# Block sums of the last feed-forward product and the last additions of the second norm: VectorE or GpSimd

## The chip, the cores and the metric

The kernel runs on one core of a Trainium2 chip. The metric is the device time of one execution in microseconds (us). Lower is better. Before the change, three executions took 989.52, 991.27 and 992.14 us; their median is 991.27 us.

## The reference, cut to what matters

One post-norm decoder layer over 1024 tokens of 1024 channels in float32. The pooling and attention mixers come first; what the change touches comes after them:

```python
h = layer_norm(DEEPNORM_ALPHA * h + mix, ln1_g[i], ln1_b[i])

ff = jnp.square(jax.nn.relu(h @ w_ff1[i])) @ w_ff2[i]          # (1024,1024)@(1024,4096)@(4096,1024)
h = layer_norm(DEEPNORM_ALPHA * h + ff, ln2_g[i], ln2_b[i])     # the second norm: (x-mean)*rstd*g + b

gate = jax.nn.sigmoid(h @ w_ple_gate[i] + b_ple_gate[i])
h = h + gate * (p[i] @ w_ple[i])
```

## The kernel before, in words

**Products in three parts.** Each float32 operand is split into a high part (a cast to `fp32r` on ScalarE, `high`, L98) and a low part (the operand minus its high part, `low`, L103, on VectorE nearly everywhere). `mm3` (L112 to L115) multiplies high by high, high by low and low by high into one PSUM bank, so each 128x512 block product is three matmuls: L113, L114, L115.

**The feed-forward's second product** is done by a Strassen-like scheme of seven products (`SEQUENCE` = 1, 5, 4, 3, 7, 6, 2). Each product runs over eight groups of hidden channels (`QORDER`), which gives 56 units, numbered 0 to 55 here. A unit is 24 matmuls of 512 columns. For unit u, `prepare(u)` makes both operands: the activation operand is a sum or a difference of two hidden blocks for the products whose first entry in `PRODUCTS` has two parts (a tile `st`, 128x1024 floats, two buffers), then split into a tile `w` (two buffers). The weight operand is read into a tile `ws`, and split into one half of a tile `x_703` (two halves in turn). `multiply(u)` then runs the 24 matmuls. The last product, number 2, is units 48 to 55, and each of its units has such a sum.

In the rows below the sums and splits of the late units are: unit 46 `st_6503`, `w_6505`; 47 `st_6536`, `w_6538`; 48 `st_6584`, `w_6586`, weights `ws_6501`; 49 `st_6617`, `w_6619`, `ws_6534`; 50 `st_6654`, `w_6656`; 51 `st_6702`; 52 `st_6750`; 53 `st_6792`; 54 `st_6855`; 55 `st_6897`.

**The second norm** (`norm2`, `layer_norm`) works on a block of 128 tokens. Statistics on VectorE (L403, L405), reciprocal root (L409 and L410 for blocks 0 to 3, GpSimd's `pow` at L412 for blocks 4 to 7), the mean taken off on ScalarE (L418), the scaling by gain on VectorE (L419), and last the addition of the bias `gb[1]` (tile `ws_6344`). Blocks 0 to 3 lie in the tile `pre_5033`, and their norms run while products 6 and 2 are multiplied; blocks 4 to 7 (`n_5251`, `n_5253`, `n_6733`, `n_6735`) follow product 2. After a block's norm, `flip` transposes it: a 32x32 transpose on VectorE (L424), a write to DRAM (L425, SP's queue) and four reads back (L427, SP's queue). The result is split and multiplied with the gate weights.

**What sets the order.** Each engine runs its instructions in the order that the scheduler of the framework gave them when the program was built; an instruction that waits holds up all behind it on its engine. GpSimd's queue also issues the transfers of L740, which add one weight block onto another.

Of the kernel before, what the change touches and what calls it, by code (L numbers as in the profile page):

```python
# [10 lines left out]
ALU = mybir.AluOpType  # L11
# [56 lines left out]
def layer(ctx, tc, xT, x, pT, w_in, w_pool, pscale, sinks, w_out, ln1, w1, w2, ln2, w_ple, w_gate, bgate, bias, rcount, out):  # L68
    nc = tc.nc
# [13 lines left out]
    def wt(shape, dt=F32R):  # L83
        return sb.tile(shape, dt, tag="w", bufs=2, name=nm("w"))
# [4 lines left out]
    def stage(shape):  # L89
        return sb.tile(shape, F32, tag="st", bufs=2, name=nm("st"))  # L90

    def small(shape):
        return cp.tile(shape, F32, tag="sm", bufs=10, name=nm("sm"))
# [23 lines left out]
    def add(o, a, b, op=ALU.add):  # L117
        nc.vector.tensor_tensor(out=o, in0=a, in1=b, op=op)  # L118
# [278 lines left out]

    hn = [None] * NT

    def layer_norm(y, gb, root=False):  # L400
        st = small([P, 2, 6])
        for i in range(2):
            nc.vector.bn_stats(out=st[:, i, :], in_=y[:, i * HALF : (i + 1) * HALF])  # L403
        mv = small([P, 8])
        nc.vector.bn_aggr(out=mv[:, 0:2], in_=st.rearrange("p a b -> p (a b)"))  # L405
        v, r0, e, r, m = (mv[:, i : i + 1] for i in range(2, 7))
        nc.vector.tensor_scalar(out=v, in0=mv[:, 1:2], scalar1=LN_EPS, scalar2=None, op0=ALU.add)
        if root:
            nc.vector.reciprocal(out=r0, in_=v)  # L409
            nc.scalar.activation(out=r0, in_=r0, func=AF.Sqrt)  # L410
        else:
            nc.gpsimd.tensor_tensor(out=r0, in0=v, in1=mhalf, op=ALU.pow)  # L412

        nc.vector.scalar_tensor_tensor(out=e, in0=r0, scalar=v, in1=r0, op0=ALU.mult, op1=ALU.mult)
        nc.vector.tensor_scalar(out=e, in0=e, scalar1=-0.5, scalar2=1.5, op0=ALU.mult, op1=ALU.add)
        nc.vector.tensor_tensor(out=r, in0=r0, in1=e, op=ALU.mult)
        nc.vector.tensor_scalar(out=m, in0=mv[:, 0:1], scalar1=-1.0, scalar2=None, op0=ALU.mult)
        nc.scalar.activation(out=y, in_=y, func=AF.Identity, bias=m, scale=1.0)  # L418
        nc.vector.scalar_tensor_tensor(out=y, in0=y, scalar=r, in1=gb[0], op0=ALU.mult, op1=ALU.mult)  # L419
        add(y, y, gb[1])  # L420

    def flip(y, b, t, d):
        b4 = b.rearrange("p (q k c) -> p q k c", q=4, k=NK)
# [115 lines left out]
    def norm1(n):  # L539
        t, c = n // 4, n % 4  # L540
        layer_norm(hn[n], gb1)
        a = transposed(hn[n], 0, tr_ps())
        b = transposed(hn[n], 1, tr_av())
        nc.scalar.mul(out=hn[n], in_=hn[n], mul=ALPHA)
        nc.scalar.dma_start(out=h_dram[n], in_=hn[n])
        if t == 0:
            if c < 3:
                nc.scalar.copy(out=pre[:, 4 + c].rearrange("p (k t) -> p k t", k=4), in_=a)
            split_to("11", c, a, nc.vector)
            split_to("21", c, b, nc.vector)  # L550
        else:
            r12, t1, t2 = temp((P, 4, P)), temp((P, 4, P)), nat([P, 4, P])
            nc.scalar.copy(out=r12, in_=a)
            if c < 3:
                add(t1, a, pre[:, 4 + c].rearrange("p (k t) -> p k t", k=4), ALU.subtract)
            else:
                for i in range(2):
                    add(t1, t1 if i else a, block("11", i, c), ALU.subtract)
            add(t2, b, t1, ALU.subtract)
            split_to("22", c, b, nc.vector)  # L560
            add(r12, b, r12, ALU.subtract)
            split_to("T1", c, t1, nc.vector)
            split_to("T2", c, t2, nc.vector)
            diff[c] = t2, split_to("T3", c, r12, nc.vector)
# [159 lines left out]
    def incoming(shape=(P, 2, HALF)):  # L724
        return part(shape, F32)
# [44 lines left out]
    def hid(q, t, k):  # L770
        return hidden[q][:, k, t] if q in hidden else FF[q, k, t]

    SIGN = {1: ALU.add, -1: ALU.subtract}
    right = wide("x7", [P, 2, 2, 2, HALF], F32R)

    def split2(s, src):
        high(s[:, 0], src)
        lows.append(low(nc.vector, s[:, 1], src, s[:, 0]))
        return s

    def prepare(u):
        i, q = units[u]
        ta = PRODUCTS[i][0]
        a = hid(q, *ta[0][:2])
        if len(ta) == 2:
            sa = stage([P, 2, HALF])
            add(sa, a, hid(q, *ta[1][:2]), SIGN[ta[1][2]])
            a = sa
        b = blocks[u]
        if len(b) == 2:  # L790
            add(b[0], b[0], b[1], ALU.subtract)
        operands[u] = split2(wt([P, 2, 2, HALF]), a), split2(right[:, u % 2], b[0])
# [11 lines left out]
    acc = []  # L804
# [36 lines left out]
        return h2  # L841

    def norm2(n):
        layer_norm(acc[n], gb2, n < 4)

    def residual_back(count):
        for n in range(len(acc), len(acc) + count):
            acc.append(nat([P, D]))
            nc.sync.dma_start(out=acc[n], in_=h_dram[n])

    prepare(0)
    banks_of, pending = {}, []
    for u, (i, q) in enumerate(units):
# [13 lines left out]
        if u + 1 < len(units):  # L867
            prepare(u + 1)
# [13 lines left out]
        if i == 6:  # L882
            if k == 0:
                gb2 = [incoming((P, D)) for _ in range(2)]
                for j in range(2):
                    nc.sync.dma_start(out=gb2[j], in_=ln2[j].partition_broadcast(P))
            if k in (3, 6):
                norm2(k // 3 - 1)
        if i == 2:
            if k in (1, 4):  # L890
                norm2(2 + k // 3)
            if k == 2:
                residual_back(2)
            if k >= 2:
                gate_load(k - 2)
            if k == 4:
                gate_flip(0)
# [5 lines left out]
    for n in range(4, NT):  # L903
        norm2(n)
# [88 lines left out]
```

## Time and profile before

| | before |
|---|---|
| median of three executions | 991.27 us (989.52 to 992.14) |
| profiled execution, its own time | 990.92 us |
| its span, first to last instruction | 989.1 us |
| TensorE (PE) busy | 980.2 us, 99% |
| VectorE (DVE) busy | 718.7 us, 73% |
| ScalarE (ACT) busy | 457.6 us, 46% |
| GpSimd (POOL) busy | 106.7 us, 11% |
| TensorE clock granted | 1.0 throughout |

The time outside the span is 990.92 - 989.1 = 1.8 us. The shares are means over the span. PE counts as busy while matmuls follow each other in its pipeline, so its idle time is read from the starts of consecutive matmuls: 512 columns start every 0.23 us where nothing holds them.

### The profile page before, as it was taken

What the parts mean: (1) busy time and instruction counts of PE and PEld (TensorE: products, weight loads), DVE (VectorE), ACT (ScalarE), POOL (GpSimd) and SP (SyncE); (2) the same over time, 40 slices, a digit from 0 to 9 for tenths busy, and PEclk for the clock granted to TensorE, in tenths of its full rate; (3) what the DMA queues carried; (4) which work ended last, traced back from release to release, by engine and by line L of the source; (5) the groups of instructions that cost most, each with busy time, mean ns of one, the idle gap of its engine ahead of it and who ended that gap; (6) DMA issues with size and microseconds to landing.
All of it is one profiled execution on the core that took longest, in us unless ns stands there. A gap on an engine that the chain in (4) does not pass through costs nothing.

```text
span 989.1 us, 12163 instructions
## 1 busy us (share of the span) xinstructions
PE 980.2 (99%) x4498; PEld 814.0 (82%) x4498; DVE 718.7 (73%) x1137; ACT 457.6 (46%) x729; POOL 106.7 (11%) x142
## 2 busy tenths in 40 slices
PE   9999999999999999999999999999999999999998
PEld 7888887888888888888888888888888888778887
DVE  5798888895869777565446856887657699899533
ACT  5676666543576434444353433433434354553111
POOL 0013552020010000100000000100011110001000
PEclk9999999999999999999999999999999999999999
DMA  6512142622161543652363893675798776652411
GB/s 219 182 64 86 44 149 86 213 84 108 64 225 74 191 149 128 201 182 107 106 246 138 318 337 110 167 238 192 204 219 195 193 177 206 211 170 104 152 43 43
DMA packets 44763, 156.39 MB, mean 158 GB/s; under 512 B 5408, under 2 KB 10656, under 8 KB 41888
## 3 DMA queue, kind: packets, MB, share of 16 engines
q1 hardware_dynamic: 35280, 124.29, 36.6%
q0 software_dynamic: 7840, 26.74, 11.3%
q10 hardware_dynamic: 1584, 4.59, 1.2%
q8 instruction: 35, 0.57, 0.2%
q14 instruction: 24, 0.20, 0.1%
HBM read 128.86 MB, written 26.74 MB: 157 GB/s over the span
## 4 chain that ended last, share of the span: by engine, by line
PE 89%; DVE 5%; DMA 3%; issue 1%; ACT 1%; SPq 0%; DVEq 0%; ACTq 0%
PE f L114 20%; PE f L115 20%; PE f L113 20%; PE mm L113 8%; PE mm L115 8%; PE mm L114 8%; DMA ws<-in_w_gate 1%; DVE x L103 1%; PE pt L317 1%; DVE w L103 1%; PE s L294 1%; DMA ws<-in_w 1%; PE s L293 1%; DVE st L118 1%; PE av L323 1%
## 5 line engine op out<-in xcount | busy, mean ns | idle before, releaser
L114 PE MATMUL f<-x,w 128*128 128x512 f32 x448 | 174.8, 390 | 1.4 <-DVE x L103 1.2
L113 PE MATMUL f<-c,ws 128*128 128x512 f32 (+1 forms) x456 | 175.7, 385 | 0.0
L114 PE MATMUL f<-c,ws 128*128 128x512 f32 (+1 forms) x456 | 175.7, 385 | 0.0
L115 PE MATMUL f<-c,ws 128*128 128x512 f32 (+1 forms) x456 | 174.9, 386 | 0.0
L115 PE MATMUL f<-x,w 128*128 128x512 f32 x448 | 174.4, 389 | 0.0
L113 PE MATMUL f<-x,w 128*128 128x512 f32 x448 | 147.1, 389 | 0.0
L98 ACT CAST w<-st 128x1024 fp32r<-128x1024 f32 (+2 forms) x66 | 65.6, 998 | 104.0 <-issue 58.0
L103 DVE TENSOR_TENSOR w<-st,w 128x1024 fp32r<-128x1024 f32 (+2 forms) x66 | 77.4, 1176 | 44.6 <-ACT w L98 44.4
L114 PEld LDWEIGHTS f<-x,w 128*128 128x128 f32 x448 | 84.1, 188 | 20.7 <-DVE x L103 3.3
L115 PEld LDWEIGHTS f<-c,ws 128*128 128x128 f32 x456 | 85.7, 188 | 17.5 <-DVE ws L103 0.4
L114 PEld LDWEIGHTS f<-c,ws 128*128 128x128 f32 x456 | 85.7, 188 | 17.2
L113 PEld LDWEIGHTS f<-c,ws 128*128 128x128 f32 x456 | 85.7, 188 | 17.2
L113 PEld LDWEIGHTS f<-x,w 128*128 128x128 f32 x448 | 84.0, 188 | 17.6 <-ACT x L98 0.2
L115 PEld LDWEIGHTS f<-x,w 128*128 128x128 f32 x448 | 84.1, 188 | 17.3
L98 ACT CAST ws<-w 128x512 fp32r<-128x512 f32 x60 | 37.1, 622 | 57.8 <-PE f L115 42.4
L103 DVE TENSOR_TENSOR x<-ws,x 128x1024 fp32r<-128x1024 f32 x52 | 63.3, 1218 | 0.0
L118 DVE TENSOR_TENSOR n<-t,f 128x512 f32<-128x512 f32 x48 | 31.8, 684 | 39.3 <-PE f L115 39.2
L103 DVE TENSOR_TENSOR ws<-w,ws 128x512 fp32r<-128x512 f32 x60 | 41.1, 688 | 24.8 <-ACT ws L98 24.4
L98 ACT CAST ws<-st 128x512 fp32r<-128x512 f32 x48 | 29.8, 621 | 60.5 <-PE f L115 35.2
L113 PE MATMUL mm<-c,w 128*128 128x512 f32 x144 | 56.7, 399 | 0.2 <-ACT w L98 0.2
L115 PE MATMUL mm<-c,w 128*128 128x512 f32 x144 | 56.6, 394 | 0.0
L114 PE MATMUL mm<-c,w 128*128 128x512 f32 x144 | 56.5, 393 | 0.0
(210 smaller groups left out, 1811.9 us busy)
## 6 DMA issues: line engine op xcount, KB each, us to landing
ws<-in_w SPq DMA_DIRECT2D x70, 512.0 KB, 3.8
w<-in_w SPq DMA_DIRECT2D x16, 1024.0 KB, 5.0
c<-fd SPq DMA_DIRECT2D x6, 2048.0 KB, 8.6
fd<-n POOLq DMA_DIRECT2D x20, 512.0 KB, 3.5
ws<-in_w POOLq DMA_DIRECT2D x20, 512.0 KB, 7.9
st<-in_w_in SPq DMA_DIRECT2D x17, 512.0 KB, 3.3
w<-in_w SPq DMA_DIRECT2D x10, 512.0 KB, 4.1
n<-in_x SPq DMA_DIRECT2D x8, 512.0 KB, 5.7
```

The costliest lines, as they stand in the source:

```text
L98: nc.scalar.copy(out=dst, in_=src)
L103: return eng.tensor_tensor(out=dst, in0=src, in1=hi.bitcast(F32), op=ALU.subtract)
L113: nc.tensor.matmul(o, ah, bh, start=first, stop=False, skip_group_check=more)
L114: nc.tensor.matmul(o, ah, bl, start=False, stop=False, skip_group_check=more)
L115: nc.tensor.matmul(o, al, bh, start=False, stop=last, skip_group_check=more)
L118: nc.vector.tensor_tensor(out=o, in0=a, in1=b, op=op)
L293: nc.tensor.matmul(s[:, i, dst], ql, kt[:, 0, g, kk : kk + kn], start=True, stop=False)
L294: nc.tensor.matmul(s[:, i, dst], ql, kt[:, 1, g, kk : kk + kn], start=False, stop=True)
L317: nc.tensor.transpose(pt[:, i, :], e[:, i, kb * P : (kb + 1) * P], ident)
L323: nc.tensor.matmul(av, VV[0][:, blk, g], pp[:, 1], start=False, stop=(kb == 1))
```

## The change

Two kinds of 128x1024 additions are given to GpSimd: the sums of hidden blocks for product 2 (eight, L787), and the bias additions of the second norm (eight, L420). All others stay on VectorE; those of the first norm go through the same line of `layer_norm` with VectorE as the default.

```diff
-    def layer_norm(y, gb, root=False):
+    def layer_norm(y, gb, root=False, eng=None):
...
-        add(y, y, gb[1])
+        (eng or nc.vector).tensor_tensor(out=y, in0=y, in1=gb[1], op=ALU.add)
...
         if len(ta) == 2:
             sa = stage([P, 2, HALF])
-            add(sa, a, hid(q, *ta[1][:2]), SIGN[ta[1][2]])
+            (nc.gpsimd if i == 2 else nc.vector).tensor_tensor(out=sa, in0=a, in1=hid(q, *ta[1][:2]), op=SIGN[ta[1][2]])
             a = sa
...
     def norm2(n):
-        layer_norm(acc[n], gb2, n < 4)
+        layer_norm(acc[n], gb2, n < 4, nc.gpsimd)
```

GpSimd's queue, the difference, from its last L740 transfer on (`ws_6467`): the sums are `st_...`, the bias additions `pre_5033`.

```order
 L740 DMA ws_6467<-in_w 128x1024
+L420 TENSOR_TENSOR pre_5033<-pre_5033,ws_6344 128x1024
+L787 TENSOR_TENSOR st_6584<-n_4580,n_4561 128x1024
+L420 TENSOR_TENSOR pre_5033<-pre_5033,ws_6344 128x1024
+L787 TENSOR_TENSOR st_6617<-n_4830,n_4795 128x1024
+L420 TENSOR_TENSOR pre_5033<-pre_5033,ws_6344 128x1024 x2
+L787 TENSOR_TENSOR st_6654<-c_4886 128x1024
+L787 TENSOR_TENSOR st_6702<-c_4923 128x1024
+L787 TENSOR_TENSOR st_6750<-c_4959 128x1024
```

The queue was empty here up to the `pow` of block 4; now the sums of units 48 and 49 stand between bias additions, and those of units 50 on stand behind all four.

VectorE's queue before, from the scaling of block 2 (`sm_6688`) to the transpose of block 2 (`n_7052`):

```order
L419 SCALAR_TENSOR_TENSOR pre_5033<-pre_5033,sm_6688,ws_6343 128x1024
L103 TENSOR_TENSOR w_6586<-st_6584,w_6586 128x1024
L415 TENSOR_SCALAR sm_6826<-sm_6826 128x1
L103 TENSOR_TENSOR x_703_4878<-ws_6501,x_703_4878 128x1024
L424 STREAM_TRANSPOSE n_6943<-pre_5033 128x1024
L118 TENSOR_TENSOR pre_5033<-pre_5033,ws_6344 128x1024
L118 TENSOR_TENSOR st_6654<-c_4886 128x1024
L416 TENSOR_TENSOR sm_6826<-sm_6826 128x1
L103 TENSOR_TENSOR w_6619<-st_6617,w_6619 128x1024
L103 TENSOR_TENSOR x_703_4878<-ws_6534,x_703_4878 128x1024
L419 SCALAR_TENSOR_TENSOR pre_5033<-pre_5033,sm_6826,ws_6343 128x1024
L424 STREAM_TRANSPOSE n_7052<-pre_5033 128x1024
```

The same place with the change, from the split of unit 47 to that of unit 49:

```order
L103 TENSOR_TENSOR w_6538<-st_6536,w_6538 128x1024
L416 TENSOR_TENSOR sm_6688<-sm_6688 128x1
L416 TENSOR_TENSOR sm_6826<-sm_6826 128x1
L103 TENSOR_TENSOR x_703_4878<-ws_6467,x_703_4878 128x1024
L419 SCALAR_TENSOR_TENSOR pre_5033<-pre_5033,sm_6688,ws_6343 128x1024
L419 SCALAR_TENSOR_TENSOR pre_5033<-pre_5033,sm_6826,ws_6343 128x1024
L424 STREAM_TRANSPOSE n_6943<-pre_5033 128x1024
L103 TENSOR_TENSOR w_6586<-st_6584,w_6586 128x1024
L103 TENSOR_TENSOR x_703_4878<-ws_6501,x_703_4878 128x1024
L424 STREAM_TRANSPOSE n_7052<-pre_5033 128x1024
L103 TENSOR_TENSOR w_6619<-st_6617,w_6619 128x1024
L103 TENSOR_TENSOR x_703_4878<-ws_6534,x_703_4878 128x1024
```

Both scalings (blocks 2 and 3) and the transpose of block 1 now stand ahead of unit 48's splits, and the transpose of block 2 stands ahead of unit 49's.

## Prediction

> **What bounds the kernel now.** I read the page first: engine shares, then the chain that ended last.
>
> ```profile
> span 989.1 us, 12163 instructions
> PE 980.2 (99%) x4498; PEld 814.0 (82%) x4498; DVE 718.7 (73%) x1137; ACT 457.6 (46%) x729; POOL 106.7 (11%) x142
> PE 89%; DVE 5%; DMA 3%; issue 1%; ACT 1%; SPq 0%; DVEq 0%; ACTq 0%
> ```
>
> TensorE is the bound: an edit on other engines pays only where matmuls now wait for what it speeds up, and costs where it makes them wait. So I looked at busy time by stretch around the moved work. Columns after the length are busy time and count for PE, PEld, DVE, ACT, POOL.
>
> ```profile
> 808.00:842.40 34.40, 33.78 (x149) 27.43 (x147) 34.40 (x48) 15.85 (x18) 0.86 (x1) 1.00 0.67 199
> 842.40:871.00 28.60, 27.90 (x121) 22.32 (x121) 24.28 (x24) 15.32 (x16) 0.00 (x0) 1.00 0.67 213
> 871.00:925.00 54.00, 54.00 (x237) 44.36 (x238) 52.50 (x86) 21.29 (x23) 4.22 (x4) 1.00 0.42 146
> ```
>
> From 808.0 to 842.4 DVE is never idle, and it feeds PE just in time. This is what it costs; the PE timeline has the three places where matmuls waited for unit 50, 52 and 55's split of weights (start, length, merged count).
>
> ```profile
> 840.71 1.07 PE L113 MATMUL f<-x,w 128*128 128x512 f32 x4
> 842.57 0.50 PE L114 MATMUL f<-x,w 128*128 128x512 f32 x1 [0.79 <-DVE x L103]
> ...
> 852.93 0.84 PE L113 MATMUL f<-x,w 128*128 128x512 f32 x3
> 853.88 0.50 PE L114 MATMUL f<-x,w 128*128 128x512 f32 x1
> ...
> 869.42 1.14 PE L113 MATMUL f<-x,w 128*128 128x512 f32 x4
> 870.98 0.50 PE L114 MATMUL f<-x,w 128*128 128x512 f32 x1 [0.42 <-DVE x L103]
> ```
>
> Matmuls start every 0.23 us. Four from 840.71 leave the next due at 841.6; it came at 842.57, 0.95 us late. By the same count the others were late by 0.27 and 0.65 us. Together 1.9 us: that is all that a relieved DVE can give back, 0.2% of the time. A measurement of this kernel tells about 0.3% (3.0 us) from no change, so a visible gain is all but excluded, and the question is what the move costs.
>
> **Price on DVE.** Its work in the first two stretches, grouped by form (count | busy, mean ns):
>
> ```profile
> L103 DVE TENSOR_TENSOR x<-ws,x 128x1024 fp32r<-128x1024 f32 x6 | 7.3, 1219 | 0.0
> L103 DVE TENSOR_TENSOR w<-st,w 128x1024 fp32r<-128x1024 f32 x6 | 7.3, 1210 | 0.0
> L118 DVE TENSOR_TENSOR pre<-pre,ws 128x1024 f32<-128x1024 f32 x4 | 4.8, 1212 | 0.0
> L118 DVE TENSOR_TENSOR st<-c 128x1024 f32<-128x1024 f32 x4 | 4.8, 1198 | 0.0
> L419 DVE SCALAR_TENSOR_TENSOR pre<-pre,sm,ws 128x1024 f32<-128x1024 f32 x3 | 3.8, 1282 | 0.0
> L424 DVE STREAM_TRANSPOSE n<-pre 128x1024 f32<-128x1024 f32 x3 | 3.7, 1241 | 0.0
> L118 DVE TENSOR_TENSOR st<-n,n 128x1024 f32<-128x1024 f32 x2 | 2.4, 1222 | 0.0
> L403 DVE BATCH_NORM_STATS2 sm<-pre 128x6 f32<-128x512 f32 x2 | 1.3, 662 | 0.0
> ```
>
> ```profile
> 841.29 1.22 DVE L103 TENSOR_TENSOR x<-ws,x 128x1024 fp32r<-128x1024 f32 x1
> 842.43 1.22 DVE L118 TENSOR_TENSOR st<-c 128x1024 f32<-128x1024 f32 x1
> ```
>
> Records overlap: one of 1.22 us takes a step of 842.43 - 841.29 = 1.14 us. In 808.0 to 842.4 the change takes away the four `pre` additions and four of the six sums (units 48 to 51; 46 and 47 belong to product 6 and stay): 8 x 1.14 = 9.1 us. DVE keeps 34.4 - 9.1 = 25.3 us.
>
> **Price on POOL.** No 128x1024 addition stands on POOL in this trace; the nearest rows are half as long.
>
> ```profile
> L103 POOL TENSOR_TENSOR c<-y,c 128x512 fp32r<-128x512 f32 x8 | 11.5, 1432 | 19.9 <-ACT c L98 19.9
> L361 POOL TENSOR_TENSOR h<-h 128x527 f32<-128x527 f32 x8 | 9.1, 1136 | 7.4 <-ACT h L353 7.4
> L103 POOL TENSOR_TENSOR wp<-st,wp 128x512 fp32r<-128x512 f32 x1 | 1.3, 1301 | 25.5 <-ACT wp L98 25.5
> L370 POOL TENSOR_TENSOR h<-h,h 128x15 f32<-128x15 f32 x1 | 0.2, 219 | 0.1
> ```
>
> With 0.2 us fixed (the 15-element row), 512 elements from two tiles at 1.30 us are 2.15 ns each, so 1024 take about 2.4 us. The cheapest form, L361 at 1.06 us for 527 elements (its row at 102.67 below), would make it 1.9 us. I take 2.4: the moved additions read two places far apart, as `wp` does, where L361 reads one tile against itself shifted by an element or a few. So POOL needs twice DVE's time, and that alone would be hidden: eight of them are 19 us in 34.
>
> It isn't alone. These rows show what POOL and DVE do to each other:
>
> ```profile
> 102.67 1.06 POOL L361 TENSOR_TENSOR h<-h 128x527 f32<-128x527 f32 x1
> 103.37 1.45 DVE L103 TENSOR_TENSOR w<-st,w 128x1024 fp32r<-128x1024 f32 x1 [2.75 <-ACT w L98]
> ...
> 182.13 1.23 DVE L103 TENSOR_TENSOR c<-st,c 128x1024 fp32r<-128x1024 f32 x1 [1.51 <-ACT c L98]
> 182.70 1.81 POOL L103 TENSOR_TENSOR c<-y,c 128x512 fp32r<-128x512 f32 x1 [10.62 <-ACT c L98]
> ...
> 217.75 1.22 DVE L103 TENSOR_TENSOR x<-n,x 128x1024 fp32r<-128x1024 f32 x1
> 217.85 2.72 POOL L412 TENSOR_TENSOR sm<-sm,mhalf 128x1 f32<-128x1 f32 x1 [4.35 <-DVE sm L417]
> 218.88 1.28 DVE L103 TENSOR_TENSOR ws<-ws,ws 128x512 fp32r<-128x512 f32 x2
> ```
>
> The DVE split that starts under POOL's addition ends at 104.82, 1.09 us after POOL ends (103.73): it stood still. The other way, POOL's addition at 182.70 ends at 184.51, 1.15 us after DVE's split ends (183.36). So an addition on POOL and a DVE operation on two SBUF tiles exclude each other, and POOL's 512 elements hold DVE off for 1.15 us; 1024 then hold it off for about 2.25 us (1.75 by L361's form). Splits and scalings read two SBUF tiles; transposes and statistics read one, and I count them as free to run beside POOL.
>
> **The sum, first stretch.** DVE's 25.3 us plus eight holds of 2.25 (18.0) are 43.3 us if none is hidden: 8.9 more than 34.4. The most that can hide lies under three transposes (3 x 1.16 = 3.5) and two statistics (2 x 0.6): 4.7 us; and unit 51's sum need not be done by 842.4. Then 25.3 + 7 x 2.25 - 4.7 = 36.4, 2.0 more. PE follows DVE here, and gets all of it: the bounds are +2.0 and +8.9, and I take the middle, +5.4, because the trace has POOL both let in early and kept out (next). The reordering adds to it: two scalings stand ahead of unit 48's splits, and the transpose of block 2 waits for a POOL addition that queues behind unit 49's sum, with unit 49's splits behind it.
>
> **Second stretch.**
>
> ```profile
> L103 DVE TENSOR_TENSOR x<-ws,x 128x1024 fp32r<-128x1024 f32 x6 | 7.3, 1218 | 0.0
> L103 DVE TENSOR_TENSOR c<-ws,c 128x1024 fp32r<-128x1024 f32 x6 | 7.2, 1220 | 4.3 <-ACT c L98 4.3
> L103 DVE TENSOR_TENSOR w<-st,w 128x1024 fp32r<-128x1024 f32 x5 | 6.1, 1218 | 0.0
> L118 DVE TENSOR_TENSOR n<-n,f 128x512 f32<-128x512 f32 x3 | 2.0, 678 | 0.0
> ```
>
> DVE keeps 17 splits, 17 x 1.14 = 19.4 us; four holds are 9.0; together 28.4 of 28.6 us (the `n` additions read one operand from PSUM and can run beside POOL). The 4.3 us for which DVE now waits for gate weights (`c`) shrinks when PE is later, and POOL can work in it. So this breaks even, and the late starts of units 52 and 55 (0.27 + 0.65 = 0.9 us) go.
>
> **After 871.** Four bias additions move, 9 us of holds for 4.6 us of DVE work, in a stretch where DVE is 52.5 of 54.0 us busy but PE does not wait. The last bias addition, and the split of block 4 that follows it on DVE:
>
> ```profile
> 915.30 1.18 DVE L118 TENSOR_TENSOR n<-n,ws 128x1024 f32<-128x1024 f32 x1
> 917.00 1.21 DVE L103 TENSOR_TENSOR ws<-n,ws 128x1024 fp32r<-128x1024 f32 x1
> ```
>
> Each block is 60 matmuls, 13.6 us, so PE needs block 4 four blocks before its end at about 984.9, at 930: 12 us of cover against some 5. Cost 0; without cover it would be those 5. SP: the reads back of block 0 and the gate loads stand behind the same transposes as before; block 2's comes some 2 us earlier in the order and later by the holds. Cost 0. POOL's `pow` for block 4 stands behind unit 55's sum, needed 20 us sooner: 0.
>
> Total: +5.4 - 0.9 = +4.5. The profiled execution took 990.92 us, 0.35 below the median: **995.4 us**. Its own range is 992.0 to 999.8.
>
> **Rivals.** *Not slower: the holds fall into gaps.* Nothing kept DVE from running three operations in a row from 217.75 to 220.2 while a POOL operation of 0.55 us waited 2.72. If POOL enters only where DVE waits or runs port-free work, and a hold is nearer 1.75, DVE's stretch is 25.3 + 7 x 1.75 - 4.7 = 32.9 us, under 34.4: PE's 1.9 us come back, 989.0. It decides when a POOL addition holds DVE off for under 1.97 us (34.4 - 25.3 + 4.7, over 7). Against it: the two-tile rows at 1.15 us per 512. Chance 0.27.
>
> *Slower still: first come, first served.* If POOL is let in after each DVE operation, each addition delays the splits in full: +8.9, 999.8, more where unit 48's splits stand behind two scalings and two additions. The row at 217.85 speaks against it, since POOL was passed over twice. Chance 0.15.
>
> [...]
>
> *Late tail.* Blocks 4 to 7 come later than PE wants them: about +5 on top, 1000. Chance 0.03.
>
> **How the numbers follow.** Forecast 0.55, rivals 0.27, 0.15, 0.03. The range for 8 in 10 takes the forecast's own, nearly all of the first rival and half of the second: 989.3 to 1000.0. Within 0.3% (988.3 to 994.2) lie the first rival but for 0.04 and a quarter of the forecast: 0.38. Slower: 0.58. Faster: 0.04.
>
> **What would show it.** POOL additions of 2.4 us or more, DVE splits of 1.8 to 3.5 us instead of 1.22 between 808 and 876, matmuls waiting for `x` or `w` at units 46 to 50 by 1 us and more, and the tail after product 2 as long as now (about 113 us). Wrong, if POOL's rows are under 2 us, if splits keep 1.22 us, or if the lateness arises after 871.

## The result, and the profile after

The changed kernel takes **998.9 us** (median of four executions, 998.60 to 999.32); the kernel before took 990.83 us in the four beside it. The ratio is 1.0082, 95% interval 1.0064 to 1.0099: slower by 8.1 us, where 4.5 were forecast. The profiled execution took 998.6 us.

The page of the changed kernel, the same lines as before; the last of them is the first group of its list, the matmuls that wait for a split of weights (busy us, mean ns, idle time ahead of them and its releaser). The single line behind it is that group before the change:

```profile
span 996.8 us, 12160 instructions
...
PE 981.7 (98%) x4498; PEld 814.5 (82%) x4498; DVE 726.1 (73%) x1121; ACT 457.9 (46%) x729; POOL 154.6 (16%) x158
...
PE 91%; DVE 6%; issue 1%; DMA 1%; ACT 0%; DVEq 0%; ACTq 0%
...
L114 PE MATMUL f<-x,w 128*128 128x512 f32 x448 | 175.9, 393 | 7.7 <-DVE x L103 7.7
```

```profile
L114 PE MATMUL f<-x,w 128*128 128x512 f32 x448 | 174.8, 390 | 1.4 <-DVE x L103 1.2
```

VectorE gave up sixteen additions and is busy for 7.4 us longer than before (726.1 against 718.7). So the operations that stayed became longer. The stretches that the prediction used show where:

```profile
808.00:842.40 34.40, 27.11 (x108) 21.00 (x107) 34.40 (x35) 11.96 (x14) 22.58 (x8) 0.90 0.54 163
842.40:871.00 28.60, 28.60 (x128) 23.68 (x127) 22.12 (x15) 13.82 (x14) 15.64 (x5) 1.00 0.56 188
871.00:925.00 54.00, 53.61 (x236) 43.73 (x235) 52.89 (x80) 23.81 (x25) 11.60 (x8) 1.00 0.42 137
```

In 808.0 to 842.4, VectorE is again never idle, with 35 instructions instead of 48, and TensorE ran 108 matmuls instead of 149. In the two later stretches matmuls flow as before. The clock column has a 0.90 that was not foreseen.

GpSimd's moved additions, grouped from 800 to 880 us, and from the timeline one that found VectorE out of its way:

```profile
L787 POOL TENSOR_TENSOR st<-c 128x1024 f32<-128x1024 f32 x6 | 19.9, 3317 | 10.3 <-DVE w L103 10.3
L420 POOL TENSOR_TENSOR pre<-pre,ws 128x1024 f32<-128x1024 f32 x4 | 12.8, 3200 | 1.2 <-DVE pre L419 1.2
L787 POOL TENSOR_TENSOR st<-n,n 128x1024 f32<-128x1024 f32 x2 | 6.8, 3410 | 9.5 <-DVE w L103 6.9 <-DVE sm L416 2.6
```

```profile
911.05 2.40 POOL L420 TENSOR_TENSOR n<-n,ws 128x1024 f32<-128x1024 f32 x1 [1.38 <-DVE sm L415]
```

Undisturbed, one takes 2.40 us, as priced. Beside VectorE the groups read 3.2 to 3.4: the addition waits for the operation that VectorE is in. Then it runs, and VectorE waits for it. The two timelines at unit 48, VectorE first, show this (start, length):

```profile
825.74 1.21 DVE L103 TENSOR_TENSOR x<-ws,x 128x1024 fp32r<-128x1024 f32 x1
826.87 4.61 DVE L419 SCALAR_TENSOR_TENSOR pre<-pre,sm,ws 128x1024 f32<-128x1024 f32 x2
831.41 1.23 DVE L424 STREAM_TRANSPOSE n<-pre 128x1024 f32<-128x1024 f32 x1
832.57 2.24 DVE L103 TENSOR_TENSOR w<-st,w 128x1024 fp32r<-128x1024 f32 x1
834.73 3.35 DVE L103 TENSOR_TENSOR x<-ws,x 128x1024 fp32r<-128x1024 f32 x1
```

```profile
825.75 3.45 POOL L787 TENSOR_TENSOR st<-n,n 128x1024 f32<-128x1024 f32 x1 [2.61 <-DVE sm L416]
830.37 6.64 POOL L420 TENSOR_TENSOR pre<-pre,ws 128x1024 f32<-128x1024 f32 x2 [1.16 <-DVE pre L419]
836.97 3.35 POOL L787 TENSOR_TENSOR st<-c 128x1024 f32<-128x1024 f32 x1
```

GpSimd's sum waits under the split that ends at 826.95, runs to 829.20, and the two scalings take 4.61 us instead of 2.4. One addition of the pair that starts at 830.37 holds the split `w`, the other the split `x`. The transpose at 831.41, which reads one tile, keeps its 1.23 us beside the first of them. Without holds the five operations from 826.87 on take 5 steps of some 1.15 us, 5.7 us; they took 11.2 (826.87 to 838.08). TensorE's timeline at the same place:

```profile
831.67 1.07 PE L113 MATMUL f<-x,w 128*128 128x512 f32 x4
838.14 0.80 PE L114 MATMUL f<-x,w 128*128 128x512 f32 x1 [5.40 <-DVE x L103]
838.74 0.63 PE L115 MATMUL f<-x,w 128*128 128x512 f32 x1
839.16 0.63 PE L114 MATMUL f<-x,w 128*128 128x512 f32 x1
...
841.29 0.63 PE L115 MATMUL f<-x,w 128*128 128x512 f32 x1
841.72 0.53 PE L113 MATMUL f<-x,w 128*128 128x512 f32 x1
842.09 0.40 PE L114 MATMUL f<-x,w 128*128 128x512 f32 x1
```

Four matmuls from 831.67 leave the next due at 832.58: it is 5.56 us late. **And the matmuls behind it start every 0.43 us instead of 0.23**, until 841.7. Nine steps from 838.14 to 842.09 take 3.95 us instead of 2.05: 1.9 us lost to a halved clock.

**The sum.** Counted from the starts of matmuls, the waits of the changed kernel are 0.36, 1.55, 0.47 and 5.56 us (units 45 to 48) and 0.55 (unit 55), 8.5 in all, where before they were 1.9: +6.6. The half clock adds 1.9. The profiled run before had lost 0.9 us more in its first 800 us. That makes +7.6; the spans differ by 7.7.

### The profile page after: what moved, and what is told of

The parts are those of the page before. It is cut to its first block, busy times and chain, and to the rows that moved or that the text cites. A ratio compares the mean times of both kernels' runs of the same rounds, so it can differ in the third digit from the quotient of the medians.

```text
span 996.8 us, 12160 instructions
## 1 busy us (share of the span) xinstructions
PE 981.7 (98%) x4498; PEld 814.5 (82%) x4498; DVE 726.1 (73%) x1121; ACT 457.9 (46%) x729; POOL 154.6 (16%) x158
## 3 DMA queue, kind: packets, MB, share of 16 engines
q0 software_dynamic: 7840, 26.74, 11.2%
## 4 chain that ended last, share of the span: by engine, by line
PE 91%; DVE 6%; issue 1%; DMA 1%; ACT 0%; DVEq 0%; ACTq 0%
PE f L114 21%; PE f L115 21%; PE f L113 20%; PE mm L113 8%; PE mm L115 8%; PE mm L114 8%; DVE x L103 2%; PE pt L317 1%; DVE w L103 1%; DMA ws<-in_w_gate 1%; PE s L294 1%; PE s L293 1%; DVE c L103 1%; PE av L323 1%; PE av L322 1%
## 5 line engine op out<-in xcount | busy, mean ns | idle before, releaser
L103 DVE TENSOR_TENSOR w<-st,w 128x1024 fp32r<-128x1024 f32 (+2 forms) x66 | 79.5, 1207 | 51.8 <-ACT w L98 51.6
L103 DVE TENSOR_TENSOR x<-ws,x 128x1024 fp32r<-128x1024 f32 x52 | 67.5, 1299 | 0.0
```

Source lines behind the costliest of these rows:

```text
L103: return eng.tensor_tensor(out=dst, in0=src, in1=hi.bitcast(F32), op=ALU.subtract)
```

## The experiments

Two theories stood: the *port* theory (a name alone, as in the prediction's "port-free work": no run shows a port), that a GpSimd addition and a VectorE operation on two SBUF tiles shut each other out, and that it costs whatever slack is lacking where this happens; and the *latency* theory, that a sum or a bias addition simply comes later from a slower engine. The first two expectations have a variant of the latter, the *queue* theory: sums come late because they stand behind bias additions in GpSimd's queue, and scalings were moved ahead of unit 48's splits. Then came a third question, what the half clock costs. In the table, waits are those of matmuls over 0.25 us between 800 and 930 us, and "half" is what the steps of 0.43 us lost. The runs came in three groups; each group had its own executions of the kernel before (medians 989.4, 990.27 and 989.6 us).

| kernel | median us | ratio to before [95%] | waits (longest), us | half, us |
|---|---|---|---|---|
| before | see above | 1 | 1.9 (0.95) | 0 |
| sums only | 995.96 | 1.0063 [1.0049, 1.0076] | 4.8 (3.80) | 3.2 |
| additions of the norm only | 996.94 | 1.0072 [1.0059, 1.0084] | 6.5 (4.80) | 3.0 |
| tail additions only | 989.61 | 1.0002 [0.9994, 1.0011] | 2.1 (0.93) | 0 |
| sums of units 52 to 55 only | 993.32 | 1.0042 [1.0029, 1.0054] | 3.7 (3.13) | 1.7 |
| before, 8 idle additions | 996.63 | 1.0068 [1.0056, 1.0080] | 7.2 (3.68) | 1.7 |
| before, 20 idle memsets | 990.27 | 0.9997 [0.9987, 1.0006] | 1.3 (0.90) | 0 |
| before, 16 idle copies | 993.54 | 1.0037 [1.0024, 1.0049] | 3.8 (2.53) | 1.6 |
| sums of units 53 to 55 only | 992.18 | 1.0019 [1.0010, 1.0028] | 3.3 (1.17) | 0 |
| changed, filler of 24 | 1000.07 | 1.0098 [1.0084, 1.0113] | 6.9 (3.70) | 2.9 |
| changed, filler of 36 | 998.88 | 1.0093 [1.0078, 1.0108] | 5.0 (2.41) | 1.7 |
| changed, filler of 56 | 997.52 | 1.0077 [1.0063, 1.0090] | 1.9 (1.40) | 0 |
| changed, again | 999.25 | 1.0094 [1.0080, 1.0108] | 9.9 (5.56) | 1.7 |

**Halves of the change.** *Sums only*: the norm's additions go back to VectorE.

```diff
-        layer_norm(acc[n], gb2, n < 4, nc.gpsimd)
+        layer_norm(acc[n], gb2, n < 4)
```

> Only the eight sums of product 2 go to GpSimd; the bias additions of the second norm stay on VectorE. Port theory (an addition on GpSimd and a VectorE operation on two SBUF tiles exclude each other, each addition holding VectorE off for 2.25 us, GpSimd let in after every VectorE operation): four holds (9.0 us) against 4.6 us of relief between 808 and 842, so +2 to +4.4 us over before, about half of the +8.1 of both moves, and splits of 2.2 to 3.4 us beside each sum. Queue theory (the loss comes from sums that stand behind bias additions in GpSimd's queue, and from scalings moved ahead of unit 48's splits): without the bias additions there is nothing to stand behind, so within 1 us of before.

*Additions of the norm only*: the sums go back.

```diff
-            (nc.gpsimd if i == 2 else nc.vector).tensor_tensor(out=sa, ...)
+            nc.vector.tensor_tensor(out=sa, ...)
```

> Only the eight bias additions go to GpSimd; the sums stay on VectorE. Port theory: again four holds against 4.6 us of relief in the stretch before 842, +2 to +4.4 us. Queue theory: the sums no longer wait for GpSimd, so within 1 us of before unless VectorE's transposes wait for the additions. If the TensorE clock drops only after a wait of several us, neither of these two shows a drop, and the two losses together come to about 2 us less than the 8.1 of both moves.

Alone, either half costs nearly what both cost: +6.6 and +7.5 us beside +8.1. Both expectations missed: the port theory had +2 to +4.4 us, the queue theory 1 us at most. The waits come near the port theory (+2.9 and +4.6 us over those before). The rest is, within some 0.5 us, the half clock (3.2 and 3.0 us), which each of the three kernels pays for once. It was granted for 6.83 us in all three, but in the changed kernel 3.0 us of that fell into the wait itself, where nothing ran that it could slow down, against 0.8 with the sums and 1.2 with the norm's additions. So the two halves don't add up, and no theory on record had the half clock in them.

**The tail alone, and late sums alone.** *Tail additions only*: as above, with `nc.gpsimd if n > 3 else None` for the norm, so blocks 4 to 7.

> Only the bias additions of blocks 4 to 7, after product 2, go to GpSimd. By the port theory VectorE loses some 4 us there, but TensorE has 10 us of cover: within 1 us of before. Rival (the tail of blocks 4 to 7 is late): +2 us and more, as matmul waits after 925.

No cost (0.9994 to 1.0011). The holds are there all the same; a 128x1 operation of 0.2 us stands under the first addition:

```profile
898.71 2.37 DVE L414 SCALAR_TENSOR_TENSOR sm<-sm 128x1 f32<-128x1 f32 x1
```

So the cover that the prediction named there is real. *Late sums*: `nc.gpsimd if u > 51 else nc.vector`, the norm on VectorE.

> Only the sums of units 52 to 55 go to GpSimd, in the stretch where VectorE already waits 4.3 us for gate weights. Port theory: four holds of 2.25 against 4.6 us of relief just fit, so within 1 us of before, at best 0.9 us faster by the waits of units 52 and 55, and gate splits of about 3.4 us. Rival (every addition moved to GpSimd costs its hold wherever it stands): +2 to +4 us as in the earlier stretch.

This one missed: +3.9 us. The first of its four sums fell on the split of unit 50, the one that was already late before. The timelines of GpSimd, VectorE and TensorE in that kernel:

```profile
839.69 3.26 POOL L787 TENSOR_TENSOR st<-c 128x1024 f32<-128x1024 f32 x1 [32.43 <-DVE w L103]
```

```profile
840.65 3.39 DVE L103 TENSOR_TENSOR x<-ws,x 128x1024 fp32r<-128x1024 f32 x1
```

```profile
844.10 0.55 PE L114 MATMUL f<-x,w 128*128 128x512 f32 x1 [2.97 <-DVE x L103]
844.44 0.63 PE L115 MATMUL f<-x,w 128*128 128x512 f32 x1
```

The split took 3.39 us instead of 1.22, the matmul was 3.13 us late instead of 0.95, and half rate followed. Here one hold of 2.2 us at a place without slack was worth 2.2 us and a drop of the clock. That reading was then tested by leaving out unit 52's sum, `nc.gpsimd if u > 52`:

> The kernel before with the sums of units 53 to 55 alone on GpSimd, none beside unit 50's split. Theory (what one GpSimd addition costs depends on the slack of the split that it holds): no wait of TensorE grows past 2 us, its clock stays at full speed, and the time is within 1 us of the kernel before, at best 0.9 us below. Rival (each addition costs whatever stands beside it): a third less than with units 52 to 55, +2 to +3 us.

It costs 1.9 us (1.0010 to 1.0028, so 1.0 to 2.8 us): the expected "within 1 us" missed, and the time lies nearer to the rival's +2 to +3. What the theory said of the wait and the clock held: the longest wait is 1.17 us, and the clock stayed full. The trace has one new wait, 1.17 us at unit 54, and 0.3 at unit 55; the three holds that are left still cost something, but the dear one, and the drop of the clock, went with unit 52's sum. So slack explains the dear hold; that a hold in this stretch is free is not shown.

**Idle work on GpSimd.** These decide between the two theories. The kernel before stays as it was, with every operation on VectorE in its order, but for two memsets far earlier. GpSimd works on scratch tiles that nothing waits for, from 808 us on. Three kinds of work, with two, no and one tile read:

```diff
+            if 48 <= u < 52:
+                with tc.issue_after(added[-1].ins):
+                    for _ in range(2):
+                        nc.gpsimd.tensor_tensor(out=idle[2], in0=idle[0], in1=idle[1], op=ALU.add)
```

with `range(5)` of `nc.gpsimd.memset(idle[2], 0.0)`, or `range(4)` of `nc.gpsimd.tensor_copy(out=idle[2], in_=idle[0])`, in its place.

> The kernel before, with VectorE keeping every operation and in its old order, plus eight GpSimd additions of 128x512 on scratch tiles that nobody waits for, queued behind the last accumulating transfer of weights, at about 808 us. Theory (each GpSimd addition excludes the VectorE operations on two SBUF tiles, and is let in after one of them): eight holds of 1.15 us are 9.2 us on a VectorE that is 34.4 of 34.4 us busy there; matmuls get between 4 and 9 us of it as lateness, splits beside the additions read 2.3 us instead of 1.22, and where one wait of TensorE passes 3 us its clock falls to half for some 4 us, 2 us more: +4 to +11 us. Rival (what costs is that moved operations get a longer latency and a second engine's semaphores, not that the engines exclude each other): nothing waits for these additions, so within 0.5 us of the kernel before.

> The same with 20 GpSimd memsets of 128x512 in place of the eight additions: GpSimd is as long in work (about 10 us), but it writes SBUF and reads nothing. If only operations that read two SBUF tiles exclude each other: within 1 us of the kernel before, VectorE's splits keep 1.22 us. If any GpSimd access to SBUF excludes VectorE's two-tile operations: as with the additions, +4 to +11 us.

> The kernel before, plus 16 GpSimd copies of 128x512 on scratch tiles in the place of the eight idle additions: they read one SBUF tile where the additions read two, and the memsets none. If GpSimd needs two SBUF tiles to shut VectorE out: as with the memsets, within 1 us of the kernel before, splits at 1.22 us. If one is enough: 16 holds of 0.6 us or more, splits above 1.5 us beside them, +3 to +9 us.

The additions cost 6.4 us, the copies 3.9, the memsets nothing. GpSimd's group in each (busy us, mean ns with the time under VectorE's operations), in the order additions, memsets, copies:

```profile
L797 POOL TENSOR_TENSOR t<-t,t 128x512 f32<-128x512 f32 x8 | 17.0, 2128 | 0.5
```

```profile
L797 POOL MEMSET t<- 128x512 f32 x20 | 10.9, 544 | 1.1
```

```profile
L797 POOL COPY t<-t 128x512 f32<-128x512 f32 x16 | 22.3, 1396 | 0.9
```

And VectorE's timeline in each, in the same order: the first split of weights behind 808 us, and the same 128x1 operation of the norm 5 to 9 us later.

```profile
813.27 2.17 DVE L103 TENSOR_TENSOR x<-ws,x 128x1024 fp32r<-128x1024 f32 x1
...
822.25 1.24 DVE L414 SCALAR_TENSOR_TENSOR sm<-sm 128x1 f32<-128x1 f32 x1
```

```profile
812.11 1.22 DVE L103 TENSOR_TENSOR x<-ws,x 128x1024 fp32r<-128x1024 f32 x1
...
817.03 0.22 DVE L414 SCALAR_TENSOR_TENSOR sm<-sm 128x1 f32<-128x1 f32 x1
```

```profile
812.96 1.50 DVE L103 TENSOR_TENSOR x<-ws,x 128x1024 fp32r<-128x1024 f32 x1
...
819.22 0.56 DVE L414 SCALAR_TENSOR_TENSOR sm<-sm 128x1 f32<-128x1 f32 x1
```

VectorE's split reads 2.17 us beside additions, 1.50 beside copies, and its usual 1.22 beside memsets. A 128x1 operation that reads two tiles, 0.2 us long, reads 1.24, 0.56 and 0.22. Nobody waited for this work, and VectorE ran the same operations in the same order as before, so the latency theory, which had 0, cannot explain these losses. In these three runs, what holds VectorE is a GpSimd operation that reads SBUF; one tile read is enough, and two make it longer: 1.0 us an addition (2.17 - 1.22), some 0.3 a copy (1.50 - 1.22), nothing a memset.

**The half clock.** If the clock falls because TensorE stands idle, work without use should keep it up. The changed kernel got transposes of the identity into a bank that is overwritten, ahead of unit 48's matmuls; 24 of them first, then 56 and 36:

```diff
+        if u == 48:
+            with tc.issue_after(ended[-1].ins):
+                for j in range(24):
+                    nc.tensor.transpose(banks_of[i][0][:, 0:P], ident, ident)
```

> The changed kernel, with 24 transposes of the identity (0.21 us each, 5.1 us) on TensorE ahead of unit 48's matmuls, into a bank that is overwritten: they fill the 5.6 us for which TensorE now waits. Theory (TensorE's clock falls to half because it stood idle for over 3 us): the granted clock stays at full speed in 836 to 843, the 1.9 us come back, less up to 0.7 us for three matmuls that no longer run ahead of the wait: 997.0 to 998.0 us where the changed kernel takes 998.9, a gain of 0.9 to 1.9 us against it. Rival (the clock falls for another reason, load or time): the clock falls all the same, and the time is that of the changed kernel or up to 1 us above it.

Missed, because the filler was mis-sized: one transpose takes 0.106 us, not 0.21, so 24 left 3.70 us of the wait. The clock fell all the same, and three matmuls that had run ahead of the wait no longer did. The next group has the right lengths, beside the changed kernel itself:

> The changed kernel with 56 transposes of the identity ahead of unit 48's matmuls. With 24 of them (0.106 us each) TensorE still stood idle for 3.7 us and its clock fell; 32 more are 3.4 us and leave under 0.5 us. Theory (the clock falls because TensorE stood idle for about 3 us or more): no matmul after the wait is 0.43 us from the next, the window 838 to 846 has a granted clock of 1.0, and the time is 2 to 3 us below that with 24 transposes (1000.1): 997 to 998. Rival (the clock falls for another reason): matmuls at half rate all the same, 1000 us.

> The same with 36 transposes: TensorE stands idle for about 2.4 us, between the longest wait after which its clock stayed (2.2 us) and the shortest after which it fell (3.1 us). If the clock falls: 999.5 to 1000.5 us, as with 24. If it stays: 997 to 998, as with 56, since the filler takes only time in which TensorE waited. No theory says which; the run places the bound.

> The changed kernel itself, as the base for the two fillers on the same chip: 998.6 to 999.3 us as measured, with a wait of 5.6 us at unit 48 and half rate for 3.7 us behind it.

The same 3.6 us with the filler of 56, with 36, and in the changed kernel as first profiled; the column behind POOL's is the granted clock:

```profile
838.20:841.80 3.60, 3.60 (x18) 2.93 (x17) 3.60 (x3) 0.00 (x0) 2.44 (x2) 1.00 0.88 266
```

```profile
838.20:841.80 3.60, 3.60 (x10) 2.86 (x11) 3.60 (x3) 0.00 (x0) 2.44 (x2) 0.57 0.70 207
```

```profile
838.20:841.80 3.60, 3.60 (x9) 2.83 (x10) 3.60 (x3) 0.00 (x0) 2.44 (x2) 0.50 0.76 220
```

With 56 the clock stays at 1.0, and the time is 997.52 us beside 999.25: the 1.7 us of the drop, as the first theory had it. With 36, TensorE missed 2.41 us and in the profiled execution the clock fell; the median is within 0.4 us of the unfilled time, and below the 999.5 to 1000.5 that was expected for a drop. Of its five executions three have a mean granted clock of 0.998 (998.88, 999.14 and 1000.41 us) and two one of 1.0 (998.47 and 998.54): at this length the clock sometimes falls (the last section says more). So idleness is the cause. It costs about a quarter of the slowdown; the holds are the rest.

## Why the prediction was right or wrong

- *TensorE is the bound, and 1.9 us is all that can come back*: right. The late starts at units 50 and 52 did go (1.2 us), and larger ones took their place.
- *Price on VectorE, price on GpSimd*: right (9.1 us of VectorE's work gone; 2.40 us for one addition).
- *The hold, 2.25 us for 128x1024*: right for a single one. The split of unit 50 grew by 2.17 us in the run with late sums.
- ***First stretch, +5.4*: mis-sized; it measured +7.0**, without the clock (waits of 7.94 us to unit 48, less the 0.95 that stood there before). The bounds +2.0 and +8.9 held it. The middle was the wrong pick, and the reason given for it was the row at 217.85, where GpSimd's 128x1 `pow` was passed over twice. The wide additions were not passed over: at 826.95, and throughout the two timelines at unit 48, each went in after the one operation that was running. In turn-taking, the rival *first come, first served* was right: there, whichever operation had begun ran to its end (the split 1.21 us, to 826.95; the sum 2.25, to 829.20), and the other waited. Why `pow` waited 2.72 us is still open (it reads 2.73 at its longest in the changed kernel too).
- *The reordering adds to it* was left without a price. It is where the longest wait arose: the two scalings ahead of unit 48's splits are the 4.61 us row, and the two bias additions behind them hold both splits.
- *Splits and scalings read two tiles* left out the norm's 128x1 operations, of which L414 is one. They are held as well: three of them took 4.2 us in 808 to 842.4, in place of 0.6 (the changed kernel first, then before).

```profile
L414 DVE SCALAR_TENSOR_TENSOR sm<-sm 128x1 f32<-128x1 f32 x3 | 4.2, 1437 | 0.0
```

```profile
L414 DVE SCALAR_TENSOR_TENSOR sm<-sm 128x1 f32<-128x1 f32 x3 | 0.6, 212 | 0.0
```

- *Transposes, statistics and operations with one operand in PSUM run free beside GpSimd*: right, by the rows of the changed kernel under GpSimd's additions. A transpose took 1.23 us (at 831.41), statistics 0.64 (at 807.27), and `t<-n,f`, with `f` in PSUM, 0.67 (at 916.46).
- ***The granted clock*: missing from the sum, +1.9.** The trace of before has a clock of 1.0 in all three stretches and no wait over 0.95 us in them, so it could not show the drop; a range that reached up to a wait of 8.9 us should have asked what TensorE does in one.
- *Second stretch, -0.9*: nearly so. Unit 52's wait went, unit 55's shrank from 0.65 to 0.55: -0.4.
- *After 871, SP and GpSimd's queue, 0*: right; the tail alone gives 1.0002, and GpSimd's hold on the split of block 4 in the changed kernel (2.91 us instead of 1.21) reached no matmul.

The forecast of 995.4 us is 3.5 under the result. In the profiled run, 7.0 - 0.4 + 1.9 - 0.9 = 7.6 stand where the prediction had 5.4 - 0.9 = 4.5. That the result still lies in the range on record is in part luck: the missing 1.9 us of the clock are as much as the holds stayed under their upper bound (8.9 - 7.0). The rival's 999.8 is nearer to the result, but for the same reason partly by accident: it put 8.9 us into holds alone.

## What to carry to other kernels

Before an operation that reads SBUF is moved from VectorE to GpSimd, compare GpSimd's time for it (here 2.40 us, twice VectorE's) with what VectorE saves: in this kernel, where VectorE was saturated with operations on two SBUF tiles, the move of one addition took 1.14 us off it and put 2.2 us of standing still on it. Move it only to places where such a hold meets slack, as in the tail here, and look first at the split that is already late. When a wait of TensorE may come near those after which its clock fell here (2.41 us and more; none up to 2.18), add a possible drop of it to the sum (here 1.6 to 3.2 us).

## What had not been expected of the hardware

- **TensorE's granted clock fell to 0.5 at every wait of 2.41 us or more in this stretch, and for 3.41 or 6.83 us.** Between 800 and 930 us of these profiles it fell at every wait of 2.41, 2.53, 3.13, 3.68, 3.70, 3.80, 4.80 and 5.56 us, and at none of the waits up to 2.18 us (that one ended at 815.5 us beside the idle additions). Every half-rate stretch there was granted for 3.41 or 6.83 us, one step or two. In the changed kernel it began at 835.17, inside the wait, and ended at 842.00; the next one, behind the last matmul, began at 995.59, 45 steps of 3.413 us later. Each drop between 800 and 930 us cost 1.6 to 3.2 us. Cut the time before it into steps of 3.41 us that end at the drop: the clock fell after every step in which TensorE was idle for 1.95 us or more, and after none in which it was idle for 1.75 us or less. The two nearest cases, the changed kernel run again and the idle additions (length, then PE's busy time; the clock is the third figure from the end):

```profile
832.63:836.05 3.42, 1.46 (x7) 0.88 (x5) 3.42 (x3) 1.99 (x2) 3.42 (x2) 1.00 0.74 238
836.05:842.87 6.82, 3.38 (x8) 2.71 (x9) 6.82 (x5) 0.00 (x0) 5.65 (x3) 0.50 0.34 97
```

```profile
811.81:815.22 3.41, 1.66 (x8) 1.05 (x6) 3.41 (x4) 2.57 (x3) 3.25 (x3) 1.00 0.25 49
815.22:818.64 3.42, 3.15 (x14) 2.62 (x15) 3.42 (x6) 0.68 (x2) 3.34 (x2) 1.00 0.46 153
```

  So the wait of 2.18 us beside the idle additions, of which 1.75 lay in one step, passed without a drop. Waits shared out in this way would explain the two executions with the filler of 36, but no trace of them shows it.
- **Losses of the parts did not add up to that of the whole.** 6.6 and 7.5 us for the halves, 8.1 for both: each of the three kernels pays once for a half clock of 6.83 us, and the longer the wait, the more of that stretch lies inside it (0.8, 1.2 and 3.0 us at waits of 3.80, 4.80 and 5.56).
- **Tiny operations paid the full hold.** A 128x1 operation of 0.2 us took 1.24 beside an idle addition (128x512), and 2.37 beside a wide one in the tail (128x1024, 2.40 us undisturbed); in these rows the length of GpSimd's operation counts, not that of VectorE's.
